# Windowed attention by half-blocks of 64 queries, two heads in one tile, inside a one-core hybrid layer

## The chip, the cores and the metric

The kernel runs on one core of a Trainium2 chip, in one launch. The core has five engines that run at the same time, each through its own instructions in a fixed order: TensorE (PE in the profile; its weight loads are listed apart as PEld), VectorE (DVE), ScalarE (ACT), GpSimd (POOL) and SyncE (SP, which here only issues DMAs). They wait for each other and for DMAs through semaphores. Data lies in SBUF (128 partitions); TensorE writes its results into PSUM. The metric is the time of one execution on the device in microseconds (us). A kernel is timed in several runs and its median is taken; one more execution is profiled, and it has its own time.

## The reference: what is computed

One layer works on 2048 latent tokens and 256 context tokens of width 1024. After a modulated normalisation one projection makes the inputs of two groups of heads: a retention of 4 heads, in chunks of 128 tokens in both directions, and an attention of 8 heads of width 64 over 2 key/value heads. An output projection, a gate, the residual and a last normalisation follow. The change is in the attention:

```python
def windowed_gqa(q, k, v, k_ctx, v_ctx, sink):
    """Latent queries: one softmax over [sink, all context keys, latent keys within +-WINDOW]."""
    G = Hq // Hkv                                   # 4 query heads share a key/value head
    qb = q.reshape(B, Hkv, G, nb, ATT_BLOCK, dh) * (dh ** -0.5)     # ATT_BLOCK = WINDOW = 128, nb = 16
    kb, vb = band_blocks(k), band_blocks(v)         # block before, own block, block after: 384 keys
    valid = (jnp.abs(qpos - kpos) <= WINDOW) & (kpos >= 0) & (kpos < L)
    s_loc = jnp.where(valid, jnp.einsum('bkgnqd,bknjd->bkgnqj', qb, kb), NEG)
    s_ctx = jnp.einsum('bkgnqd,bkcd->bkgnqc', qb, k_ctx)            # 256 context keys
    p = sink_softmax(jnp.concatenate([s_ctx, s_loc], axis=-1), sink)
    out = p[..., :Lc] @ v_ctx + p[..., Lc:] @ vb    # (einsum)
```

A query at place i of its block sees the keys from i to i+256 of the 384. So the first 64 queries of a block together see keys 0 to 319 and the last 64 see keys 64 to 383.

## The kernel before, in words

**Stages.** Up to about 660 us the kernel loads and modulates the inputs and makes the projections, which it writes to DRAM block by block (a block is 128 tokens): `d_k` keys, `d_v` values, `d_aq` queries, `d_qkv` and `d_st` for the retention, `d_g` gates. Then the last projection (`ag1` of the first four blocks) is interleaved with the attention scores of block 0 and the retention of block 0 (`WEAVE`, about 665 to 686 us). From there to 1142 us runs the block loop: 32 half-blocks t, with block b = t // 2 and key/value head kv = t % 2. The last 7 us finish block 15.

**Precision.** A value is kept as a rounded high part and a low part; the matmuls on them run on float32r (written f32 in the profile, like plain float32). Keys: each of two matmuls (`hl`) takes 128 rows of high and low parts. Transposes and the retention's matmuls are plain float32.

**One head of attention** (`att_head`, lines 713 to 749). With the 128 queries of a head as stationary operand (`AQ[b][:, h, :]`) TensorE makes the scores `S` in four matmuls: line 733 over the keys of the window in `kwin` (384 columns, 256 for blocks 0 and 15), line 737 over the 256 context keys `kctx`, each for two parts. `S` is one PSUM tile (`pS`, one buffer): the next head's scores wait until VectorE has read it. VectorE adds the mask and takes the maximum (line 739, 640 columns), ScalarE takes the exponential with its sum (line 746), and `att_norm` multiplies by the reciprocal on GpSimd (line 755) in `pb`, which holds the four heads of one kv.

**From p to the output** (`att_t`, `att_v`, lines 1186 to 1208). For each of five tiles of 128 keys (three of the window, two of the context: X and Y) TensorE transposes the four heads' probabilities (line 1193, four transposes into one PSUM bank `pt`), ScalarE makes the high part (line 1195), VectorE the low part (line 1196), both in the tile `phl` (two buffers), and TensorE multiplies with the values in two matmuls of 512 columns into `o` (line 1206). `att_out` adds the two parts of the values and multiplies by the gate, and `proj` (line 1243, tiles `pz`) is the output projection, from `mr` (retention) and `ma` (attention).

**The order** of the block loop is written out in two strings, `STEPS`, for kv = 0 and 1: a0 to a3 are the heads of the next half-block (t + 1), N their norms, T and V transposes and value matmuls of this one, o pieces of the projection, s/S, R, Y, U, q the retention of block b + 1 and its parts (`Y` writes `yt`, whose product with the gate tile `gr` becomes `mr`). t = 0 has a string of its own, `FIRST`, without heads. A list scheduler then places the instructions of each engine, the DMA issues of SP among them; it follows the strings except where it takes an operand to be late.

**Loads.** `kwin` has three slots, block b in slot b % 3; `load_kv(b + 2)` stands at the start of half-block 2b + 1, and the slot of kv is free when the last head of kv that reads the old block is done. `load_att` loads the queries of a block in four DMAs (128 KB each, runs of 512 bytes) into `aq`, two buffers. `first` holds block 0's retention inputs; `fw` is the last norm's weight.

## Time and profile before

| | |
|---|---|
| runs | 1152.22, 1150.06, 1148.82 us; median 1150.06 |
| the profiled execution | 1151.04 us, its span in the profile 1149.2 us |
| TensorE clock granted | 0.991 of full speed over the span |
| PE busy | 1129.1 us (98%), 6319 matmul records |
| PEld, DVE, ACT, POOL busy | 976.0 (85%), 786.7 (68%), 475.8 (41%), 328.3 us (29%) |
| window scores (line 733) | 224 records of 384 columns, 32 of 256 |
| context scores (line 737) | 256 records of 256 columns |
| transposes of p (line 1193) | 624 records |
| value matmuls (line 1206) | 312 records of 512 columns |

How to read it: PE's matmuls are pipelined, so a record's duration (say 338 ns) is longer than the distance to the next record's start; what a matmul costs is read from the starts of neighbours in a timeline. "Idle before" is the time in which an engine waited, with what ended it. The share of an engine is a mean over stages, so the stage in question has to be read by itself.

### The profile page before, as it was taken

How to read it: one execution, taken by the hardware profiler on the slowest of the kernel's cores; microseconds unless marked ns; L12 is line 12 of the kernel's file. 1: busy time of each engine (PE TensorE's matmuls, PEld its weight loads, DVE VectorE, ACT ScalarE, POOL GpSimd, SP SyncE). 2: the span in 40 equal slices, each digit the busy share in tenths (PEclk: the TensorE clock that was granted, in tenths of full speed). 3: DMA queues.
4: the chain of work that ended last, by engine and by line, in shares of the span. 5: the costliest groups of instructions: out<-in, count | busy, mean ns of one | idle time of the engine just before them, and what ended most of it. 6: DMA issues, size and time to landing. Idle time of an engine off the chain costs nothing.

```text
span 1149.2 us, 18100 instructions
## 1 busy us (share of the span) xinstructions
PE 1129.1 (98%) x6319; PEld 976.0 (85%) x6319; DVE 786.7 (68%) x1907; ACT 475.8 (41%) x1044; POOL 328.3 (29%) x459
## 2 busy tenths in 40 slices
PE   8999999999999999999999999999999999999997
PEld 5887879989978889998888877888888888888885
DVE  6973994665674545656657357777777777777774
ACT  4344522332453002322111156555555555555553
POOL 0000020100011200001104343555555555555553
PEclk8999999999999999999999999999999999999999
DMA  8948893374674532543356276344444444444310
GB/s 319 340 152 263 290 282 132 116 256 126 203 230 137 154 109 83 178 123 113 101 162 210 79 188 223 116 133 134 133 133 134 133 134 133 133 133 134 97 56 37
DMA packets 139537, 182.25 MB, mean 159 GB/s; under 512 B 11315, under 2 KB 103091, under 8 KB 139318
## 3 DMA queue, kind: packets, MB, share of 16 engines
q1 hardware_dynamic: 124372, 173.46, 48.0%
q10 hardware_dynamic: 15074, 7.64, 2.2%
q8 instruction: 50, 0.82, 0.3%
q14 instruction: 41, 0.34, 0.1%
HBM read 130.19 MB, written 50.86 MB: 158 GB/s over the span
## 4 chain that ended last, share of the span: by engine, by line
PE 81%; DVE 7%; issue 5%; DMA 4%; ACT 2%; POOL 1%; SPq 0%; POOLq 0%; DVEq 0%; ACTq 0%
PE pz L1243 14%; PE rv L344 8%; PE rk L331 7%; PE o L1206 6%; PE ag L331 6%; PE pt L1193 5%; PE aq L331 5%; PE rg L331 4%; PE rq L331 4%; PE S L733 3%; PE S L737 2%; PE u L460 2%; PE ak L331 2%; PE av L331 1%; DVE wss L205 1%
## 5 line engine op out<-in xcount | busy, mean ns | idle before, releaser
L746 ACT ACTIVATE p<-p,m 128x641 f32<-128x641 f32 (+1 forms) x128 | 104.6, 817 | 62.1 <-DVE m L743 61.8
L755 POOL TENSOR_SCALAR p<-p,m 128x640 f32<-128x640 f32 (+1 forms) x128 | 101.7, 794 | 87.5 <-DVE m L754 86.2
L1195 ACT ACTIVATE phl<-pt 128x512 fp32r<-128x512 f32 x156 | 92.6, 595 | 78.1 <-PE pt L1193 76.0
L1196 DVE TENSOR_TENSOR phl<-pt,phl 128x512 fp32r<-128x512 f32 x156 | 106.3, 683 | 24.1 <-ACT phl L1195 23.4
L739 DVE CUSTOM_DVE_ANT_0 p<-S,msk 128x640 f32<-128x640 f32 (+1 forms) x128 | 102.5, 801 | 13.4 <-PE S L737 6.6
L1243 PE MATMUL pz<-wg1h,ma 128*128 128x512 f32 x256 | 106.1, 419 | 0.1
L1243 PE MATMUL pz<-wg0h,mr 128*128 128x512 f32 x256 | 103.6, 409 | 0.6 <-DVE mr L113 0.6
L1193 PE MATMUL pt<-ident,p 128*128 128x128 f32 x624 | 93.2, 272 | 0.0
L1193 PEld LDWEIGHTS pt<-ident,p 128*128 128x128 f32 x624 | 75.3, 140 | 8.4
L733 PE MATMUL S<-kwin,aq 128*128 128x384 f32 (+1 forms) x256 | 79.4, 332 | 0.1
L436 ACT ACTIVATE vw<-v,wdec 128x128 fp32r<-128x128 f32 x128 | 43.7, 394 | 84.2 <-DVE v L449 84.2
L737 PE MATMUL S<-kctx,aq 128*128 128x256 f32 x256 | 71.1, 281 | 0.0
L1206 PE MATMUL o<-phl,vwin 128*128 128x512 f32 x184 | 62.2, 416 | 1.3 <-DVE phl L1196 0.8
L1243 PEld LDWEIGHTS pz<-wg0h,mr 128*128 128x128 f32 x256 | 48.1, 188 | 9.2 <-DVE mr L113 0.9
L1243 PEld LDWEIGHTS pz<-wg1h,ma 128*128 128x128 f32 x256 | 48.2, 188 | 7.8 <-POOL ma L1221 0.5
L733 PEld LDWEIGHTS S<-kwin,aq 128*128 128x128 f32 x256 | 48.0, 188 | 6.9 <-DVE m L739 1.6
L737 PEld LDWEIGHTS S<-kctx,aq 128*128 128x128 f32 x256 | 48.2, 188 | 5.2
L1243 PE MATMUL pz<-wg0l,mr 128*128 128x512 f32 x128 | 50.6, 395 | 0.0
L1243 PE MATMUL pz<-wg1l,ma 128*128 128x512 f32 x128 | 50.3, 393 | 0.0
L438 DVE SCALAR_TENSOR_TENSOR vw<-v,wdec,vw 128x128 fp32r<-128x128 f32 x128 | 40.2, 358 | 6.7 <-ACT vw L436 6.7
L1217 DVE TENSOR_TENSOR mf<-o,ob 64x256 f32<-64x256 f32 x64 | 26.7, 417 | 24.4 <-ACT ob L1214 23.8
L1206 PE MATMUL o<-phl,vctx 128*128 128x512 f32 x128 | 41.6, 404 | 0.2 <-DVE phl L1196 0.2
(425 smaller groups left out, 3015.3 us busy)
## 6 DMA issues: line engine op xcount, KB each, us to landing
wss<-in_wss SPq DMA_DIRECT2D x32, 512.0 KB, 6.1
qkv<-d_qkv SPq DMA_DIRECT2D x15, 768.0 KB, 4.8
aq<-d_aq SPq DMA_DIRECT2D x64, 128.0 KB, 3.5
xb<-in_xn SPq DMA_DIRECT2D x16, 512.0 KB, 3.7
out<-xb SPq DMA_DIRECT2D x31, 256.0 KB, 4.9
st<-d_st SPq DMA_DIRECT2D x15, 512.0 KB, 6.8
d_g<-g ACTq DMA_DIRECT2D x28, 256.0 KB, 2.8
x<-in_xt SPq DMA_DIRECT2D x12, 512.0 KB, 5.7
```

The source lines that it names most:

```text
L331: pe.matmul(ps, w[:, a, k, c0 : c0 + P], ht[b][:, k, :], start=(k == 0 and i == 0), stop=(k == NK - 1 and i == 2),)
L344: pe.matmul(ps, ht[a][:, k, t * P : (t + 1) * P], w[:, b, k, :], start=(k == 0 and i == 0), stop=(k == NK - 1 and i == 2),)
L733: i = pe.matmul(psc[:, o:512].rearrange("p (s t) -> p s t", t=P), AQ[b][:, h, :], C2["kwin"][:, kv, hl, ksel], start=(hl == 0), stop=(hl = ...
L737: pe.matmul(psc[:, 512:768], AQ[b][:, h, :], C2["kctx"][:, kv, hl], start=(hl == 0), stop=(hl == 1))
L739: dve.tensor_tensor_reduce(out=pb[:, j, 0:n], in0=psc[:, o : o + n], in1=mk, op0=ALU.add, op1=ALU.max, scale=1.0, scalar=-3e38, accum_out= ...
L746: act.activation(pb[:, j, 0 : n + 1], pb[:, j, 0 : n + 1], AF.Exp, bias=m4[:, 1, j : j + 1], scale=0.125, accum_out=m4[:, 2, j : j + 1],)
L755: PE["norm"] = pool.tensor_scalar(pb[:, j, 0:n], pb[:, j, 0:n], m4[:, 2, j : j + 1], 0.0, op0=ALU.mult, op1=ALU.add)
L1193: pe.transpose(ppt[:, j], pb[:, j, kt * P : (kt + 1) * P], ident)
L1195: PE["phl"] = act.activation(phl[:, 0], ppt, AF.Copy)
L1196: PE["low"] = dve.tensor_tensor(phl[:, 1], ppt, phl[:, 0], op=ALU.subtract)
L1206: pe.matmul(PO[kv], vt, PH[kt][:, hl], start=(kt == 0 and hl == 0), stop=(kt == nkt - 1 and hl == 1))
L1243: pe.matmul(PZ[n2], m[:, a, k % RH, :], WG[k // 4][c][:, k % 4, s], start=(k == 0 and i == 0), stop=(k == NK - 1 and i == 2),)
```

## The change

**What it does.** Attention goes by halves of a block: a unit is 64 queries of two heads (128 rows) where it was 128 queries of one head. Per block and kv there are still four units, j = 0 to 3: `sub` = j // 2 is the half, `pair` = j % 2 the pair of heads. A half has the 320 window keys that its queries can see: the own block C, the full neighbour F (128 keys) and half of the other neighbour H (64 keys). So a unit has 576 columns and not 640 (blocks 0 and 15: 448 or 512 where it was 512).

- `kwin` has five slots instead of three, so that the window of a unit is one run of columns; every third block the two blocks that are still needed are loaded again into slots 0 and 1 (four more DMAs of 128 KB). In `load_kv` the values are now loaded first.
- In `att_t` the tiles are C, F, H, X, Y; the H tile takes four transposes of 64 columns each (before: 128), and its high and low parts go into a tile of its own, `phh`, whose upper 64 rows are zero. Blocks 0 and 15 have five tiles, F and H with two transposes each (before: four tiles of four).
- In `att_v` the tiles F and H use other values for each half, so each of their matmuls of 512 columns becomes two of 256. H of the second half needs the last 64 keys of block b - 1 in partitions 0 to 63: `vs`, loaded once a block (`load_vs`, step "v").
- The queries are loaded half by half: eight DMAs of 64 KB a block, with runs of 256 bytes. The mask is a strip `msk` of 2112 columns, the sinks are set by halves of the partitions, twice a kv.
- To make room, `glast` (the last gate before its activation) takes one of the two `aq` buffers. `aq1` then takes the buffer of `aq0` and can be loaded when block 0's last head is done, `aq2` when the gate of `glast` is stored. `fw` is loaded after the weave and not in the tables' stage.

```diff
-    "a0 o0 O T0 o1 a1 N0 T1 R F0 F1 V0 a2 N1 T2 B V1 o2 a3 N2 T3 o3 V2 o4 T4 r2 N3 o5 V3 o6 V4 o7",
+    "a0 o0 O T0 o1 a1 N0 T1 R F0 F1 V0 a2 N1 T2 B V1 o2 a3 N2 T3 o3 V2 v o4 T4 r2 N3 o5 V3 o6 V4 o7",
 ...
+    def window(b, sub):
+
+        w = [("F", 0, P), ("C", P, P), ("H", 2 * P, 64)] if sub == 0 else [("H", 64, 64), ("C", P, P), ("F", 2 * P, P)]
+        return w[(b == 0) : 3 - (b == NB - 1)]
+
+    def columns(b, sub):
+
+        at, n = {}, 0
+        for name, _, m in window(b, sub):
+            at[name] = (n, m)
+            n += m
+        return {**at, "X": (n, P), "Y": (n + P, P)}, n + CTX
 ...
-    def load_kv(b):
-        if b >= NB:
-            return
+    def load_keys(s, b, n):
         for kv in range(2):
             for dup in range(2):
                 nc.sync.dma_start(
-                    C2["kwin"][64 * dup : 64 * dup + 64, kv, :, b % 3, :].bitcast(F32),
-                    d_k[kv, :, :, b * P : (b + 1) * P].rearrange("s d t -> d s t"),
+                    C2["kwin"][64 * dup : 64 * dup + 64, kv, :, s * P : (s + n) * P].bitcast(F32),
+                    d_k[kv, :, :, b * P : (b + n) * P].rearrange("s d t -> d s t"),
                 )
-        v = C2["pool"].tile([P, 2, P], F32R, tag="v", name=f"vwin{b}", bufs=4)
-        nc.sync.dma_start(v.bitcast(F32), d_v[b])
-        VW[b] = v
+
+    def load_kv(b):
+
+        w = (b - 1) % 3
+        if b < NB:
+            v = C2["pool"].tile([P, 2, P], F32R, tag="v", name=f"vwin{b}", bufs=4)
+            nc.sync.dma_start(v.bitcast(F32), d_v[b])
+            VW[b] = v
+        if w == 0 and b > 1 and b <= NB:
+            load_keys(0, b - 2, 2)
+        if b < NB:
+            load_keys(w + 2 if b else 1, b, 1)
+
+    def load_vs(b):
+
+        if b < NB:
+            nc.sync.dma_start(C2["vs"][0:64].bitcast(F32), d_v[b - 1, 64:P])
 ...
-        AQ[b] = C2["pool"].tile([P, AH, P], F32R, tag="aq", name=f"aq{b}")
-        for i in range(4):
-            nc.sync.dma_start(
-                AQ[b][32 * i : 32 * i + 32].bitcast(F32), d_aq[b, i].rearrange("g (j d) t -> d (g j) t", d=32)
-            )
+
+        AQ[b] = C2["pool"].tile([P, 2, AH, 64], F32R, tag="aq", name=f"aq{b}")
+        for sub in range(2):
+            for i in range(4):
+                nc.sync.dma_start(
+                    AQ[b][32 * i : 32 * i + 32, sub].bitcast(F32),
+                    d_aq[b, i, :, :, 64 * sub : 64 * sub + 64].rearrange("g (j d) t -> d (g j) t", d=32),
+                )
 ...
-        slots = window(b)[0]
-        nl = len(slots) * P
+        sub, pair = j // 2, j % 2
+        win = window(b, sub)
+        nl = sum(m for _, _, m in win)
         n = nl + CTX
         o = 512 - nl
-        h = 4 * kv + j
-        ksel = {0: slice(0, 2), NB - 1: slice(0, 3, 2)}.get(b, slice(0, 3))
-        m0 = mask_at(b)
-        mk = C2["msk"][:, m0 : m0 + n // P].rearrange("p s t -> p (s t)")
+        c0 = b % 3 * P + win[0][1]
 ...
-            pool.tensor_copy(PB[(b, kv)][0][:, :, n], sink8[:, 4 * kv : 4 * kv + 4])
+        if pair == 0:
+            pool.tensor_copy(pb[:, j : j + 2, n], sink8[:, 2 * kv : 2 * kv + 2])
+        h = 2 * kv + pair
+        q = AQ[b][:, sub, 2 * h : 2 * h + 2].rearrange("p h t -> p (h t)")
 ...
         for hl in range(2):
-            i = pe.matmul(
-                psc[:, o:512].rearrange("p (s t) -> p s t", t=P),
-                AQ[b][:, h, :], C2["kwin"][:, kv, hl, ksel], start=(hl == 0), stop=(hl == 1),
-            )
-            pe.matmul(psc[:, 512:768], AQ[b][:, h, :], C2["kctx"][:, kv, hl], start=(hl == 0), stop=(hl == 1))
+            i = pe.matmul(psc[:, o:512], q, C2["kwin"][:, kv, hl, c0 : c0 + nl], start=(hl == 0), stop=(hl == 1))
+            pe.matmul(psc[:, 512:768], q, C2["kctx"][:, kv, hl], start=(hl == 0), stop=(hl == 1))
 ...
-        fw = new("fw", [P, D])
-        nc.sync.dma_start(fw, fnw)
 ...
-        new("glast", [P, 2, GT])
+        C2["glast"] = c2.tile([P, 2, GT], F32, tag="aq", name="glast")
 ...
-    fw, vctx = C2["fw"], C2["vctx"]
+    vctx = C2["vctx"]
+    fw = s2.tile([P, D], F32, name="fw", bufs=1)
+    nc.sync.dma_start(fw, fnw)
+
+
+    for n, shape in (("vs", [P, 2, P]), ("phh", [P, 2, 4, P])):
+        C2[n] = s2.tile(shape, F32R, name=n, bufs=1)
+        pool.memset(C2[n].bitcast(F32), 0.0)
 ...
+    TILES = "CFHXY"
+
+    def halves_of(b, kt):
+
+        return [sub for sub in range(2) if TILES[kt] in columns(b, sub)[0]]
 ...
-        for j in range(4):
-            pe.transpose(ppt[:, j], pb[:, j, kt * P : (kt + 1) * P], ident)
-        phl = s2.tile([P, 2, 4, P], F32R, tag="phl", name=f"phl{b}_{kv}_{kt}", bufs=2)
-        PE["phl"] = act.activation(phl[:, 0], ppt, AF.Copy)
-        PE["low"] = dve.tensor_tensor(phl[:, 1], ppt, phl[:, 0], op=ALU.subtract)
+        subs = halves_of(b, kt)
+        for sub in subs:
+            c, m = columns(b, sub)[0][TILES[kt]]
+            for j in (2 * sub, 2 * sub + 1):
+                pe.transpose(ppt[:m, j], pb[:, j, c : c + m], ident)
+        phl = C2["phh"] if m < P else s2.tile([P, 2, 4, P], F32R, tag="phl", name=f"phl{b}_{kv}_{kt}", bufs=2)
+        js = slice(2 * subs[0], 2 * subs[-1] + 2)
+        PE["phl"] = act.activation(phl[:m, 0, js], ppt[:m, js], AF.Copy)
+        PE["low"] = dve.tensor_tensor(phl[:m, 1, js], ppt[:m, js], phl[:m, 0, js], op=ALU.subtract)
 ...
-        slots = window(b)[0]
-        nkt = len(slots) + 2
         if kt == 0:
             PO[kv] = bank(f"o{b}_{kv}", "o")
-        vt = VW[slots[kt][1]][:, kv, :] if kt < len(slots) else vctx[:, kt - len(slots), kv, :]
-        for hl in range(2):
-            pe.matmul(
-                PO[kv], vt, PH[kt][:, hl], start=(kt == 0 and hl == 0), stop=(kt == nkt - 1 and hl == 1)
-            )
+        t = TILES[kt]
+        if t in "CXY":
+            vt = VW[b][:, kv, :] if t == "C" else vctx[:, "XY".index(t), kv, :]
+            uses = [(vt, slice(0, 4))]
+        else:
+            near = {("F", 0): lambda: VW[b - 1], ("F", 1): lambda: VW[b + 1], ("H", 0): lambda: VW[b + 1],
+                    ("H", 1): lambda: C2["vs"]}
+            uses = [(near[(t, sub)]()[:, kv, :], slice(2 * sub, 2 * sub + 2)) for sub in halves_of(b, kt)]
+        for vt, js in uses:
+            for hl in range(2):
+                pe.matmul(
+                    PO[kv][:, js], vt, PH[kt][:, hl, js], start=(kt == 0 and hl == 0), stop=(kt == 4 and hl == 1)
+                )
```

**How it moves instructions.** In the rows below a name is the tile written, with block and kv or tile number, `<-`, the operands, and partitions x columns; xN are N equal rows in a run.

TensorE in half-block 0, after the transposes of block 0's first kv (`o0_0` their value matmuls, `pz0` the projection from `mr0`, `S1` scores of block 1). Before:

```order
L1206 MATMUL o0_0_6481<-phl0_0_2_6489,vctx_6030 128x512 x2
L1206 MATMUL o0_0_6481<-phl0_0_3_6503,vctx_6030 128x512
L733 MATMUL S1_1_6575<-kwin_6005,aq1_6449 128x384
L737 MATMUL S1_1_6575<-kctx_6017,aq1_6449 128x256
L733 MATMUL S1_1_6575<-kwin_6005,aq1_6449 128x384
L737 MATMUL S1_1_6575<-kctx_6017,aq1_6449 128x256
L1206 MATMUL o0_0_6481<-phl0_0_3_6503,vctx_6030 128x512
L1243 MATMUL pz0_0_6551<-wg0h_5749,mr0_6470 128x512
L1243 MATMUL pz0_0_6551<-wg0l_5750,mr0_6470 128x512
L1243 MATMUL pz0_1_6667<-wg0h_5749,mr0_6470 128x512
L1243 MATMUL pz0_1_6667<-wg0l_5750,mr0_6470 128x512
L733 MATMUL S1_2_6610<-kwin_6005,aq1_6449 128x384
```

And now:

```order
L1263 MATMUL o0_0_6503<-phl0_0_3_6522,vctx_6043 128x512 x2
L1263 MATMUL o0_0_6503<-phl0_0_4_6532,vctx_6043 128x512 x2
L1304 MATMUL pz0_0_6584<-wg0h_5751,mr0_6494 128x512
L1304 MATMUL pz0_0_6584<-wg0l_5752,mr0_6494 128x512
L1304 MATMUL pz0_1_6697<-wg0h_5751,mr0_6494 128x512
L1304 MATMUL pz0_1_6697<-wg0l_5752,mr0_6494 128x512
L1304 MATMUL pz0_0_6584<-wg0h_5751,mr0_6494 128x512 x2
L1304 MATMUL pz0_0_6584<-wg0l_5752,mr0_6494 128x512
L1304 MATMUL pz0_0_6584<-wg0h_5751,mr0_6494 128x512 x2
L1304 MATMUL pz0_0_6584<-wg0l_5752,mr0_6494 128x512
L1304 MATMUL pz0_0_6584<-wg0h_5751,mr0_6494 128x512 x2
L1304 MATMUL pz0_0_6584<-wg0l_5752,mr0_6494 128x512
```

The heads S1_1 and S1_2 (and S1_0, which stood ahead of pt0_0_0) are gone from here. Behind the last row come s1, the transposes of kv 1 and y1; S1_0_0 stands after y1, and S1_0_1 to S1_1_3 follow, the last four with three to six other rows between two of them.

TensorE around the third tile's transposes of a half-block in the middle (block 9, kv 1; now `pt9_1_2` are the H transposes). Before:

```order
L1193 MATMUL pt9_1_2_9697<-ident_66,p9_1_9433 128x128 x4
L1206 MATMUL o9_1_9684<-phl9_1_1_9663,vwin10_9259 128x512 x2
L1243 MATMUL pz9_0_9624<-wg0h_5749,mr9_9529 128x512
L1243 MATMUL pz9_0_9624<-wg0l_5750,mr9_9529 128x512
L1243 MATMUL pz9_0_9624<-wg0h_5749,mr9_9529 128x512
L733 MATMUL S10_3_9721<-kwin_6005,aq10_9261 128x384
```

And now:

```order
L1243 MATMUL pt9_1_2_9862<-ident_66,p9_1_9589 64x128 x4
L1263 MATMUL o9_1_9848<-phl9_1_1_9827,vwin8_8686 128x256 x2
L1263 MATMUL o9_1_9848<-phl9_1_1_9827,vwin10_9398 128x256 x2
L1304 MATMUL pz9_0_9788<-wg0h_5751,mr9_9685 128x512
L1304 MATMUL pz9_0_9788<-wg0l_5752,mr9_9685 128x512
L1304 MATMUL pz9_0_9788<-wg0h_5751,mr9_9685 128x512
L767 MATMUL S10_0_3_9887<-kwin_6007,aq10_9408 128x320
```

The second tile's two value matmuls of 512 columns have become four of 256 at the same place; the next head follows three projection matmuls later, as before, now with 320 columns. Every tile F and H of blocks 1 to 14 goes like this.

SP's queue around the keys of block 6 (`vs` and `kwin` the loads of the change, `gr6` the gate tile that takes the buffer of `gr4`). Before:

```order
L660 DMA kwin_6005<-d_k_62 64x2x128 x2
L665 DMA vwin6_7887<-d_v_63 128x256
L712 DMA xb4_7552<-in_xn 128x1024
L709 DMA ga5_7894<-d_g_64 128x512
L676 DMA st5_7783<-d_st_65 128x1024
L660 DMA kwin_6005<-d_k_62 64x2x128 x2
L696 DMA aq6_7889<-d_aq_61 32x8x128
L682 DMA gr6_7785<-d_g_64 128x512
L696 DMA aq6_7889<-d_aq_61 32x8x128 x3
```

And now:

```order
L701 DMA qkv6_7799<-d_qkv_60 128x1536
L745 DMA xb4_7630<-in_xn 128x1024
L706 DMA st5_7866<-d_st_65 128x1024
L712 DMA gr6_7868<-d_g_64 128x512
L686 DMA vwin6_7970<-d_v_63 128x256
L676 DMA kwin_6007<-d_k_62 64x2x128 x4
L728 DMA aq6_7976<-d_aq_61 32x8x64 x8
```

Before, the four key loads of a block stood in two pairs: kv 0 ahead of `vwin`, kv 1 ahead of `aq` and `gr`. Now the four of block 6 stand together behind `gr6`. So do those of blocks 4 (with the four loads of 128 KB) and 5; from block 8 on they stand ahead of `gr`, and for block 7 `gr7` stands between the two of kv 0.

More of the change, by code (lines that the diff above doesn't have):

```diff
@@ L282, in decays @@
         dve.tensor_tensor(lg, t8, u8, op=ALU.subtract)
-        dve.tensor_scalar(nsink, pr[:, 8:16], -1.0, None, op0=ALU.mult)
-        dve.tensor_scalar(sink8, pr[:, 8:16], 8.0, None, op0=ALU.mult)
+        for i in range(2):
+            rows = slice(64 * i, 64 * i + 64)
+            dve.tensor_scalar(nsink[rows], pr[rows, 8 + i : 16 : 2], -1.0, None, op0=ALU.mult)
+            dve.tensor_scalar(sink8[rows], pr[rows, 8 + i : 16 : 2], 8.0, None, op0=ALU.mult)
         for h in range(RH):
@@ L833, in new @@
             return C2[n]
-        new("kwin", [P, 2, 2, 3, P], F32R)
+        new("kwin", [P, 2, 2, 5 * P], F32R)
         load_kv(0)
@@ L852, in tables @@
             nc.sync.dma_start(vctx[:, t].bitcast(F32), d_v[NB + t])
-        fw = new("fw", [P, D])
-        nc.sync.dma_start(fw, fnw)
-        msk = new("msk", [P, 14, P], BF16)
+        msk = new("msk", [P, MASKL[1] + P + 64 + CTX], BF16)
         pool.memset(msk, 0.0)
-        for i, o in enumerate(MASKS):
-            if o != 1:
-                dve.tensor_copy(msk[:, i], tb[1][:, o // 2])
-        new("glast", [P, 2, GT])
+        for name, sub, _, _, o, n in parts:
+            for b, first_ in ((1, MASK0[sub]), (NB - 1, MASKL[sub])):
+                at = columns(b, sub)[0].get(name)
+                if at:
+                    dve.tensor_copy(msk[:, first_ + at[0] : first_ + at[0] + n], tri[:, o : o + n])
+        C2["glast"] = c2.tile([P, 2, GT], F32, tag="aq", name="glast")
         dmat = new("dmat", [P, RH, P])
```

55 lines of the change are left out of this document (31 added, 24 removed).

## The prediction

> **What bounds the kernel now.** I read the windows by stage first, then the waits, then single rows of the timeline. In the block loop the windows are, in columns: stretch, its length, busy time and count of PE, PEld, DVE, ACT and POOL, the granted clock, DMA share and GB/s.
>
> ```profile
> 700.00:800.00 100.00, 99.13 (x603) 87.70 (x604) 76.71 (x228) 56.55 (x115) 52.70 (x76) 1.00 0.44 135
> 800.00:900.00 100.00, 100.00 (x610) 88.78 (x610) 80.13 (x232) 60.77 (x126) 55.52 (x78) 1.00 0.44 132
> ```
>
> TensorE is busy without a hole, at full clock, and VectorE, the next, is at 80%. So in the loop an instruction of TensorE counts in full, and time saved on another engine counts for nothing while TensorE does not wait for it. Where it does wait is the way into the loop (the waits of PE from 660 to 712 us: total, times, longest):
>
> ```profile
> PE s L780 <- DMA first<-d_qkv: 1.3, 1, 1.3
> PE y L788 <- DVE m L754: 1.0, 1, 1.0
> PE pz L1243 <- DVE mr L113: 0.6, 1, 0.6
> PE o L1206 <- DVE phl L1196: 0.5, 2, 0.2
> PE o L1206 <- ACT phl L1195: 0.4, 1, 0.4
> ```
>
> These 3.8 us are all there is to win or lose by order. A matmul's price is the distance between starts, here one head, four transposes and three projection matmuls:
>
> ```profile
> 747.49 0.34 PE L733 MATMUL S<-kwin,aq 128*128 128x384 f32 x1
> 747.67 0.28 PE L737 MATMUL S<-kctx,aq 128*128 128x256 f32 x1
> 747.79 0.34 PE L733 MATMUL S<-kwin,aq 128*128 128x384 f32 x1
> 747.96 0.28 PE L737 MATMUL S<-kctx,aq 128*128 128x256 f32 x1
> 748.08 0.60 PE L1193 MATMUL pt<-ident,p 128*128 128x128 f32 x4
> 748.43 0.48 PE L1243 MATMUL pz<-wg1h,ma 128*128 128x512 f32 x1
> 748.75 0.39 PE L1243 MATMUL pz<-wg1l,ma 128*128 128x512 f32 x1
> 748.98 0.40 PE L1243 MATMUL pz<-wg1h,ma 128*128 128x512 f32 x1
> ```
>
> 384 columns cost 0.175 us (mean of 0.18 and 0.17), 256 cost 0.12 (over many such pairs 0.117), 512 cost 0.23. From the first transpose to the second 512 are 0.67 us: 0.231 for the first 512 leaves 0.109 for a transpose. A head costs 0.59 us.
>
> **The change part by part.**
>
> *Scores.* The two groups that set the counts here and for the transposes:
>
> ```profile
> L733 PE MATMUL S<-kwin,aq 128*128 128x384 f32 x224 | 70.8, 338 | 0.0
> L1193 PE MATMUL pt<-ident,p 128*128 128x128 f32 x624 | 93.2, 272 | 0.0
> ```
>
> 224 matmuls go from 384 to 320 columns, half way between 0.117 and 0.175, so 0.146: 224 x 0.029 = **-6.5 us**. In blocks 0 and 15 sixteen matmuls go from 256 to 192 columns. No row shows this type under 256 columns. By the line 192 would cost 0.09, which saves 0.4; at the other bound the matmul runs like the plain f32 passes of the retention, which go twice over their operands at 0.11 us for 128 columns each (rows below), so 192 cost 0.33: +3.4 us. The nearest row is the 256-column one, so I stay near the lower end and take **+0.5**.
>
> *Values.* In 28 half-blocks the tiles F and H have eight matmuls of 256 for four of 512: 8 x 0.117 against 4 x 0.231 is 0.012 us, hence +0.3; with a spread of 0.12 for a 256, at most +1.0. I take **+0.4**. Blocks 0 and 15 do in five tiles what they did in four, with as many columns.
>
> *Transposes.* There are as many as before, but 120 of them (4 in each of 28 half-blocks, 2 in four) have 64 stationary columns, with the same 128 moving ones (`ident`). Nothing in the trace has 64. What holds a transpose at 0.109 us?
>
> ```profile
> 843.27 0.39 PE L788 MATMUL y<-st,qd 128*128 128x128 f32 x2
> 843.49 0.39 PE L789 MATMUL y<-st,qd 128*128 128x128 f32 x2
> 100.35 0.47 PE L168 MATMUL ss_xc<-ones,sqc 128*128 128x1 f32 x3
> 100.68 0.47 PE L331 MATMUL rg<-h2h,wrg 128*128 128x512 f32 x1
> L1193 PEld LDWEIGHTS pt<-ident,p 128*128 128x128 f32 x624 | 75.3, 140 | 8.4
> L1243 PEld LDWEIGHTS pz<-wg0h,mr 128*128 128x128 f32 x256 | 48.1, 188 | 9.2 <-DVE mr L113 0.9
> ```
>
> Plain f32 passes of 128 moving columns are 0.11 apart (two in 0.22), and so are three passes of one single moving column (0.33): for those the load of the 128 stationary columns alone takes 0.11. But the load of a transpose is another one: its record is 140 ns where others have 188, so it is some 50 ns shorter, and if it takes 0.06 it cannot hold the transpose at 0.109. Then the moving columns do, and these stay 128: **0**. If the load holds it after all, half the columns save up to 0.053 each: 120 x 0.053 = -6.4 us. This is a rival below.
>
> The Trainium skill, page "TensorE: Matmul & The Clock Gate", section "LDWEIGHTS (loading the stationary operand)", lets the load take the stationary columns divided by 1.2 GHz, an estimate of 107 ns for 128 and 53 for 64. The one-column passes agree with it (0.11), the shorter record of the transposes speaks against it there. By that rule the sum below would be 6.4 us lower.
>
> *Other engines.*
>
> ```profile
> L739 DVE CUSTOM_DVE_ANT_0 p<-S,msk 128x640 f32<-128x640 f32 (+1 forms) x128 | 102.5, 801 | 13.4 <-PE S L737 6.6
> L746 ACT ACTIVATE p<-p,m 128x641 f32<-128x641 f32 (+1 forms) x128 | 104.6, 817 | 62.1 <-DVE m L743 61.8
> L1196 DVE TENSOR_TENSOR phl<-pt,phl 128x512 fp32r<-128x512 f32 x156 | 106.3, 683 | 24.1 <-ACT phl L1195 23.4
> ```
>
> The mask, the exponential and the norm on GpSimd shrink by a tenth, 128 times each: some 10 us on each of three engines, all under TensorE's 100%, so 0; they only make later waits less likely. The extra sinks and the two memsets stand on GpSimd at 55%: 0.
>
> *Loads in the loop.* Per block four more query DMAs, one `vs`, and every third block four of 128 KB for the keys. The queue's rows around the end of an even half-block:
>
> ```profile
> 747.38 0.69 DVE L1229 TENSOR_TENSOR gr<-yt,gr 128x512 f32<-128x512 f32 x1
> 748.86 1.30 POOL L1232 TENSOR_TENSOR mr<-gr,mr 128x512 fp32r<-128x512 f32 x1
> 748.15 1.23 SPq L660 DMA_DIRECT2D kwin<-d_k  x2
> 750.19 0.33 SPq L682 DMA_DIRECT2D gr<-d_g  x1
> 750.57 1.41 SPq L696 DMA_DIRECT2D aq<-d_aq  x3
> 753.32 0.34 PE L733 MATMUL S<-kwin,aq 128*128 128x384 f32 x1
> kwin<-d_k SPq DMA_DIRECT2D x52, 64.0 KB, 2.3
> aq<-d_aq SPq DMA_DIRECT2D x52, 128.0 KB, 3.5
> ```
>
> `gr` waits for GpSimd's `mr` (750.16) and now the keys of blocks 4, 5 and 6 stand behind it. After `gr` come `vwin` (0.33, some 0.1 to the next) and two key DMAs of 0.62: the second is issued at 751.3 and lands 2.3 later, at 753.6, while the next half-block's first scores stand at 753.32. For blocks 4 and 5 TensorE's order has put these scores much later (S3_0_0 and S4_0_0 stand behind y3 and most of y4, 2.7 us and more), for block 7 one pair is ahead; so only S5_0_0 meets it: **+0.4**, no gain possible; with the whole DMA late, 2. Queries are loaded a block ahead of use and eight issues of 0.47 with 3.5 to landing end long before: 0, and without that cover each late microsecond would stand on TensorE 14 times. `vs` waits for the H matmuls of the odd half and is wanted half a half-block later, about 10 us against 2.4: 0.
>
> *The way into the loop.* S0_0_0 waits for the first loads; four more query DMAs (0.47 each) ahead of them make it later by 1 to 2 us, which the 1.3 us wait for `first` absorbs, since `fw` (512 KB) is no longer ahead of `first`: 0, between -1.3 and +1.
>
> Then come the heads of block 1:
>
> ```profile
> 686.05 0.33 PE L733 MATMUL S<-kwin,aq 128*128 128x384 f32 x1
> 686.61 1.65 ACT L814 ACTIVATE first<-first,ra 128x128 f32<-128x128 f32 x4 [3.01 <-DVE ra L807]
> 689.55 0.43 SPq L682 DMA_DIRECT2D gr<-d_g  x1
> 696.01 0.33 PE L733 MATMUL S<-kwin,aq 128*128 128x384 f32 x1
> 696.79 0.83 DVE L739 CUSTOM_DVE_ANT_0 p<-S,msk 128x640 f32<-128x640 f32 x1 [0.40 <-PE S L737]
> 700.87 0.46 PE L788 MATMUL y<-sfw,qd 128*128 128x128 f32 x2 [0.96 <-DVE m L754]
> ```
>
> Before, three heads stood ahead of y1 (from 686.05). Now none does. The time to y1 hardly shortens by their 1.8 us where the wait is for ACT's line 814 (until 688.26), but the two masks no longer stand ahead of `mr` and of the low parts on DVE, nor the norms ahead of y1's `qd` on GpSimd. I put y1 1.6 us earlier than 700.87, with 1.1 us less of TensorE's rows done by then (the three heads gone, more projection done): **-0.5**. The queries of block 1 are issued behind `gr1` (690.0), six of 0.47, so by 692.8, and land 3.5 us later; S1_0_0 stands some 3 us behind y1, at 702: no wait.
>
> The heads then follow each other closely. A head's turn, from its first score to the end of its mask, took 1.61 us (696.01 to 697.62); with 64 columns less 1.47. From S1_1_0 to S1_1_1 there are 1.09 us of TensorE's rows, to S1_1_2 0.86: 0.4 and 0.6 are missing. S3_0_0 to S3_1_0 and S4_0_0 to S4_0_3 stand 1.55 to 1.7 apart, enough for the mask but not always for a low part (683 ns) as well: 0.8 more. Together **+1.8**. After S5 the spacing is that of before.
>
> *Sum:* -6.5 + 0.5 + 0.4 + 0 + 0.4 - 0.5 + 1.8 = -3.9. From the profiled execution's 1151.0 that gives 1147.1; the median of the runs lies 1.0 lower than that execution, so 1146.1 in the same terms. I say **1146.5**.
>
> **The rivals.**
>
> *Half transposes cost half.* For it: an f32 load of 128 columns is seen to hold 0.11 us, and the transposes stand at 0.109. Against it: their load record is shorter. It adds -6.4 (-4.8 if the last of each four is still held by the next matmul's load): 1140.
>
> *The backlog costs more (the slower side).* The heads of blocks 1, 3 and 4 are held by VectorE's whole turn, mask, two small instructions and a low part (about 0.75 + 0.3 + 0.68) behind the scores, 2.2 us instead of 1.47. Fourteen gaps from S1_0_0 to S4_0_3 are shorter than that, by 8.3 us together. For it: VectorE at 80% has no room to do twice its heads. Against it: the low parts can go first or wait in their two buffers. Price 8.3 for 1.8: +2.6, so 1152.7 by the median; it decides once more than 5.7 of the 8.3 are paid, and with 192 columns at the upper bound as well it is 1155.6.
>
> *The gain is given back without loss:* 192 columns at the upper bound (+2.9 over my value) or keys late in several blocks, 3 us: about 1149.5.
>
> **How the numbers follow.** Forecast 0.47, half transposes 0.28, given back 0.13, backlog 0.12. The range for 8 in 10 goes from the rival below, 1139.5, to the backlog, 1153; the forecast's own is 1144 to 1149. A difference of 0.3%, 3.4 us, is what this measurement can tell from none. Faster by more: the half transposes and somewhat over half of the forecast, 0.53. Within: the rest of the forecast, the gain given back and half of the backlog, 0.35. Slower: 0.12.
>
> **What would show it.** Scores of 320 columns 0.146 apart, and 192 not far above 0.1. H transposes spaced 0.109: right; 0.06: the rival. PE's waits from 660 to 720 us in sum 4 to 7 us, the new ones at lines 767 and 768 from DVE; a wait of S5_0_0 for `kwin` of about half a microsecond, and none for `aq` or `vs`. From 820 us on PE at 100% as before. The prediction is wrong where PE waits for keys in every block, or where VectorE's share in the loop does not fall below 80%.

## The result, and the profile after

The changed kernel takes **1157.9 us** (median of four runs, 1157.36 to 1158.69), the kernel before 1150.2 us beside it. The ratio is **1.0071**, interval 1.0058 to 1.0083: slower by 0.7%. The prediction was 1146.5, range 1139.5 to 1153. It was wrong, and on the wrong side.

The loss has one place. Below is the table by stage of the changed kernel, with the columns of the prediction's first view (stretch, its length, busy time and count of PE, PEld, DVE, ACT, POOL, then clock, DMA share, GB/s):

```profile
690.00:720.00 30.00, 27.69 (x158) 21.57 (x158) 18.55 (x53) 16.05 (x31) 10.26 (x16) 1.00 0.74 230
720.00:780.00 60.00, 56.56 (x351) 48.23 (x352) 44.04 (x130) 32.23 (x67) 31.17 (x48) 1.00 0.40 124
780.00:840.00 60.00, 58.59 (x371) 50.96 (x371) 46.45 (x138) 33.99 (x72) 30.99 (x48) 1.00 0.45 139
840.00:900.00 60.00, 60.00 (x388) 53.60 (x387) 47.32 (x144) 36.04 (x77) 31.16 (x49) 1.00 0.47 146
```

In the kernel before the two middle stretches were:

```profile
720.00:780.00 60.00, 60.00 (x366) 53.22 (x365) 47.70 (x141) 35.93 (x74) 33.12 (x47) 1.00 0.44 132
780.00:840.00 60.00, 60.00 (x369) 53.35 (x368) 47.55 (x137) 35.35 (x72) 33.17 (x47) 1.00 0.47 138
```

So PE was full from 720 us on, and now it is full only from 840 us on. (Its count of matmuls is higher there, 388 in 60 us for 367 before, mainly because eight value matmuls of 256 columns stand where four of 512 stood.) To put the loss into blocks I use the first transpose `yt` of each block, which stands at the same place of the program in all kernels, and the time from one to the next, each from the one profiled execution:

| us | `yt` 0 at | 0 to 1 | 1 to 2 | 2 to 3 | 3 to 5 | 5 to 15 | 15 to end | span |
|---|---|---|---|---|---|---|---|---|
| before | 687.2 | 29.9 | 28.8 | 28.8 | 57.7 | 287.8 | 29.0 | 1149.2 |
| after | 686.8 | 32.7 | 31.9 | 31.4 | 59.6 | 284.8 | 29.8 | 1156.9 |

Up to block 0 nothing is lost (-0.3). From block 0 to block 5 it is +10.2, from block 5 to block 15 -3.0 (a block of the loop is 28.46 where it was 28.83), and behind the last `yt` +0.8: together the 7.7 of the spans. So the static gain is there, block by block, and the first five blocks eat it up three times over.

What PE waited for from 665 to 845 us (total, times, longest):

```profile
PE pt L1243 <- POOL p L786: 1.8, 3, 1.1
PE S L767 <- DVE m L770: 1.6, 4, 0.6
PE S L767 <- DMA kwin<-d_k: 1.4, 2, 0.8
PE o L1263 <- DVE mf L1275: 0.9, 1, 0.9
PE o L1263 <- DVE phl L1247: 0.7, 3, 0.2
PE o L1263 <- ACT phl L1246: 0.6, 1, 0.6
PE pz L1304 <- DVE mr L114: 0.6, 1, 0.6
PE pz L1304 <- DVE mr L1293: 0.5, 1, 0.5
PE yt L1288 <- ACT first L845: 0.5, 1, 0.5
```

These rows are 8.6 us; before, all waits of that stretch were 3.8. The new ones are TensorE waiting for the heads' own chain: the mask's maximum (VectorE), the norm (GpSimd), the sum of the parts (VectorE). A wait also costs more than its length. The longest one, with the three transposes ahead of it:

```profile
727.70 0.49 PE L1243 MATMUL pt<-ident,p 128*128 128x128 f32 x3
729.33 0.33 PE L1243 MATMUL pt<-ident,p 128*128 128x128 f32 x1 [1.14 <-POOL p L786]
```

From the first of the three to the fourth it is 1.63 us, where transposes 0.11 apart take 0.33: 1.30 lost for a wait of 1.14.

The first head of block 1 stood at 686.05 before. Now (its row, and the view of the tile `aq` from 684 to 696 us, which holds only the eight loads of `aq1`):

```profile
704.27 0.31 PE L767 MATMUL S<-kwin,aq 128*128 128x320 f32 x1
...
L728 SPq DMA_DIRECT2D aq<-d_aq x8: 303/507/957, 684.6 to 694.6; - x8
...
DMA to landing us min/median/max: 1.9/5.6/7.7
```

The queries were issued from 684.6 to 694.6, and the last landing on record is at 699.3 (two of the eight have none on record). The head does not wait for them: it stands at 704.27 because in PE's order it stands behind y1, the retention of block 1. Two different things are thus late: the queries, and the order.

### The profile page after: what moved, and what is told of

It reads as the page before. It is cut to its first block, busy times and chain, and to the rows that moved or that the text cites. A ratio compares the mean times of both kernels' runs of the same rounds, so it can differ in the third digit from the quotient of the medians.

```text
span 1156.9 us, 18517 instructions
## 1 busy us (share of the span) xinstructions
PE 1130.2 (98%) x6438; PEld 974.5 (84%) x6439; DVE 782.7 (68%) x1914; ACT 469.5 (41%) x1048; POOL 328.7 (28%) x493
## 4 chain that ended last, share of the span: by engine, by line
PE 73%; DVE 10%; issue 6%; POOL 4%; DMA 3%; ACT 3%; SPq 1%; POOLq 0%; ACTq 0%; DVEq 0%
PE pz L1304 12%; PE rv L347 8%; PE rk L334 7%; PE ag L334 5%; PE o L1263 5%; PE aq L334 5%; PE pt L1243 4%; PE rg L334 4%; PE rq L334 4%; PE S L767 3%; PE S L768 2%; PE u L463 2%; PE ak L334 2%; PE av L334 1%; DVE wss L206 1%
## 5 line engine op out<-in xcount | busy, mean ns | idle before, releaser
L777 ACT ACTIVATE p<-p,m 128x577 f32<-128x577 f32 (+2 forms) x128 | 98.1, 766 | 72.0 <-DVE m L774 71.0
L786 POOL TENSOR_SCALAR p<-p,m 128x576 f32<-128x576 f32 (+2 forms) x128 | 95.8, 749 | 91.6 <-DVE m L785 84.2
L770 DVE CUSTOM_DVE_ANT_0 p<-S,msk 128x576 f32<-128x576 f32 (+2 forms) x128 | 94.3, 737 | 18.3 <-PE S L768 13.4
L1247 DVE TENSOR_TENSOR phl<-pt,phl 128x512 fp32r<-128x512 f32 x128 | 86.7, 680 | 27.6 <-ACT phl L1246 25.4
L1246 ACT ACTIVATE phl<-pt 128x512 fp32r<-128x512 f32 x128 | 75.1, 589 | 72.0 <-PE pt L1243 70.2
L1243 PE MATMUL pt<-ident,p 128*128 128x128 f32 (+1 forms) x624 | 95.4, 273 | 2.0 <-POOL p L786 1.8
L1243 PEld LDWEIGHTS pt<-ident,p 128*128 128x128 f32 (+1 forms) x624 | 74.4, 134 | 13.1 <-POOL p L786 3.4
L767 PE MATMUL S<-kwin,aq 128*128 128x320 f32 (+2 forms) x256 | 73.9, 310 | 3.6 <-DVE m L770 2.1
L767 PEld LDWEIGHTS S<-kwin,aq 128*128 128x128 f32 x256 | 48.1, 188 | 12.4 <-DVE m L770 4.5
L1263 PE MATMUL o<-phl,vwin 128*128 128x512 f32 (+1 forms) x184 | 45.2, 345 | 2.6 <-DVE phl L1247 1.0
```

Of the source, the lines that this page charges most:

```text
L767: i = pe.matmul(psc[:, o:512], q, C2["kwin"][:, kv, hl, c0 : c0 + nl], start=(hl == 0), stop=(hl == 1))
L770: dve.tensor_tensor_reduce(out=pb[:, j, 0:n], in0=psc[:, o : o + n], in1=mask(b, sub), op0=ALU.add, op1=ALU.max, scale=1.0, scalar=-3e38, ...
L777: act.activation(pb[:, j, 0 : n + 1], pb[:, j, 0 : n + 1], AF.Exp, bias=m4[:, 1, j : j + 1], scale=0.125, accum_out=m4[:, 2, j : j + 1],)
L786: PE["norm"] = pool.tensor_scalar(pb[:, j, 0:n], pb[:, j, 0:n], m4[:, 2, j : j + 1], 0.0, op0=ALU.mult, op1=ALU.add)
L1243: pe.transpose(ppt[:m, j], pb[:, j, c : c + m], ident)
L1246: PE["phl"] = act.activation(phl[:m, 0, js], ppt[:m, js], AF.Copy)
```

## The experiments

The ratio of each run is to the kernel before, timed on the same chip; the rounds ran on different chips, so between rounds the ratios are to be compared, not the times. "By the table" means the columns `0 to 1`, `1 to 2`, `2 to 3` and `3 to 5` above, in this order (six numbers: `5 to 15` and `15 to end` as well). S1_0_0 is the first unit of the scores of block 1, key/value head 0.

### First round: the shared buffer, or the key loads?

The two candidates were the buffer that `glast` takes from the queries, and the eight key loads of every third block. Run 1 gives `glast` its own tile; for its 4 KB the padded tile `phh` had to go, so run 2 has that second edit alone.

```diff
-        C2["glast"] = c2.tile([P, 2, GT], F32, tag="aq", name="glast")
+        new("glast", [P, 2, GT])
 # runs 1 and 2: no phh, and vs on 64 rows
-        phl = C2["phh"] if m < P else s2.tile([P, 2, 4, P], F32R, tag="phl", ...)
+        phl = s2.tile([P, 2, 4, P], F32R, tag="phl", ...)
-                    PO[kv][:, js], vt, PH[kt][:, hl, js],
+                    PO[kv][:, js], vt[:m], PH[kt][:m, hl, js],     # m = 64 for H
```

> The changed kernel with two edits: `glast` has a tile of its own again, so `aq1` need not wait for block 0's heads nor `aq2` for the store of the gate; and, to find its 4 KB, the H tile uses the common `phl` and its value matmuls take 64 rows, so that the padded tile `phh` is gone. Theory A (the shared buffer): all that is lost between the first `yt` of block 0 (686.8, 0.3 us ahead of the kernel before) and that of block 5 (842.3, 9.9 us behind), with the gain of five blocks some 12 us, comes from the queries of block 1 being late and VectorE's and GpSimd's work with them, the later order of blocks 2 to 5 included. Then S1_0_0 stands at about 687 (704.3 now), `yt` of block 5 at 831 to 833, and the time is 1145 to 1147. Theory B (the key loads: eight at once in every third block, behind `gr`): only the loss up to block 1, some 3 us, comes back: 1154 to 1156, with the waits of S3, S4 and S5 as they are.

Measured: 1159.8 us, ratio 1.0087 (1.0073 to 1.0101).

> The second edit of that kernel alone: H's value matmuls on 64 rows, no `phh`, `glast` still in a buffer of the queries. Both theories: no change against the changed kernel, 1156.5 to 1159. If 64 rows are cheaper or dearer than 128 padded ones for TensorE (8 matmuls of 256 columns in a half-block's F and H, 4 of them H, at 0.117 us), it shows as a spacing other than 0.117 and as up to 120 x 0.06 = 7 us.

Measured: 1168.8 us, ratio 1.0173 (1.0154 to 1.0192). Both times fell outside what either theory gave, since the edit meant as a filler costs some 11 us by itself (below, run 8). Taken against each other, the own tile is worth 9.0 us, and by the table the first head of block 1 is back at 686.0 and the blocks take 29.6, 30.3, 30.0, 58.5 in place of 32.9, 31.9, 32.7, 60.5.

Runs 3 and 4 put one part each into the kernel before: the shared buffer, and the loads (five slots, the change's `load_keys` and `load_kv`, `fw` later).

```diff
 # run 3
-        new("glast", [P, 2, GT])
+        C2["glast"] = c2.tile([P, 2, GT], F32, tag="aq", name="glast")
 # run 4, beside load_keys and load_kv
-        new("kwin", [P, 2, 2, 3, P], F32R)
+        new("kwin", [P, 2, 2, 5 * P], F32R)
-                AQ[b][:, h, :], C2["kwin"][:, kv, hl, ksel], ...
+                AQ[b][:, h, :], C2["kwin"][:, kv, hl, c0 : c0 + nl], ...     # c0 = (b % 3 + (b == 0)) * P
```

> The kernel before with one line of the change: `glast` takes one of the two `aq` buffers. Keys, heads and values are those of before. Theory A: block 1's heads stand behind y1 as in the changed kernel (S1_0 from 686.1 to about 703), VectorE is in arrears, and the kernel is slower by 3 to 7 us: 1153 to 1157. Theory B: the lateness is taken up by VectorE's reserve of 20%, at most +2: 1150 to 1152.

Measured: 1150.3 us, ratio 1.0007 (0.9997 to 1.0017).

> The kernel before with the loads of the change alone: five slots of keys, two blocks of keys loaded again in every third block (four DMAs of 128 KB), values ahead of the keys, `fw` loaded after the weave; the order on TensorE stays that of before. (The mask has 9 tiles in place of 14, since the window's blocks now stand in order.) Theory A: 1149 to 1151, with at most 0.5 us of waits for `kwin`. Theory B: waits for `kwin` or `aq` in blocks 3 to 5 and behind, slower by 4 us or more: 1154 and up.

Measured: 1149.3 us, ratio 0.9997 (0.9987 to 1.0008). The key loads cost nothing: by the table 29.9, 28.8, 28.8, 57.7, as before. But neither does the shared buffer in the kernel before (30.4, 28.8, 28.8, 57.7): there the first head of block 1 also comes late, at 698.6, near the end of y1, and 0.5 us is lost in that block and nothing behind it. So theory A did not hold as I had put it. Something else has to come with the sharing.

### Second round: the sharing with the eight query loads

Run 5 leaves the changed kernel as it is, but finds 4 KB for `glast` elsewhere: `junk` is a throw-away of the last norm that nobody needs before block 1.

```diff
-        C2["glast"] = c2.tile([P, 2, GT], F32, tag="aq", name="glast")
+        C2["glast"] = c2.tile([P, 2, GT], F32, tag="junk", name="glast", bufs=1)
-        junk = s1.tile([P, D], F32, tag="junk", name=f"junk{b}", bufs=1)
+        junk = C2["pool"].tile([P, D], F32, tag="junk", name=f"junk{b}", bufs=1)
```

> The changed kernel with one edit: `glast` takes the buffer of `junk` (a throw-away of the last norm, 4 KB, first used in block 1), which moves from the pool `s1` into the tables' pool; the query loads get both `aq` buffers as before the change, and `phh` stays with its 128 rows. Theory A (the shared buffer makes the loss): S1_0_0 at about 686, `yt` of block 5 at 831 to 833, a block of 28.46 us in the loop, and 1143 to 1147. Theory B (the loss lies in the half-block units themselves or their key loads): 1152 or more.

Measured: 1147.95 us, ratio 0.9992 (0.9982 to 1.0003). By the table 29.6, 29.7, 29.4, 56.9: 9.9 of the lost us are back, the loop block is 28.46, but the time is 1 us above the forecast; 2 us are still lost in blocks 1 to 3.

Runs 6 and 7 take the queries in halves of 64 (eight DMAs, runs of 256 bytes) into the kernel before, with and without the shared buffer.

```diff
-        for i in range(4):
-            nc.sync.dma_start(AQ[b][32 * i : 32 * i + 32].bitcast(F32), d_aq[b, i].rearrange(...))
+        for sub in range(2):
+            ts = slice(64 * sub, 64 * sub + 64)
+            for i in range(4):
+                nc.sync.dma_start(AQ[b][32 * i : 32 * i + 32, :, ts].bitcast(F32), d_aq[b, i, :, :, ts].rearrange(...))
```

> The kernel before with two lines of the change: `glast` in one of the `aq` buffers, and the queries of a block in eight DMAs of half a block (runs of 256 bytes). Heads, keys and values are those of before. Theory A1 (the shared buffer alone was 1.4 us; with eight loads, most of them queued behind others, the heads of blocks 1 to 3 come so late and close together that TensorE waits for VectorE and GpSimd): slower by 5 to 9 us, 1154 to 1158. Theory A2 (the shared buffer is dear only with the work of the half-block units): 1149 to 1152.

Measured: 1159.2 us, ratio **1.0089** (1.0071 to 1.0108).

> The kernel before with the queries in eight DMAs of half a block, nothing else. Theory A1: the loads are early enough by themselves, 1148 to 1151. If the eight loads alone are the cause, it stands where the run with both lines stands, 1154 to 1158.

Measured: 1150.3 us, ratio 1.0006 (0.9997 to 1.0014). So each of the two lines costs about 1 us by itself (0.07% and 0.06%), which this measurement does not tell from nothing, and both together cost 10, with full heads of 128 queries and 384 keys. That is a loss of the size of the changed kernel's, made without its attention. The stage table of run 6 and its new waits:

```profile
720.00:780.00 60.00, 55.92 (x329) 47.00 (x329) 45.16 (x132) 33.21 (x69) 30.30 (x43) 1.00 0.38 117
780.00:840.00 60.00, 60.00 (x368) 53.38 (x367) 47.74 (x140) 36.70 (x77) 32.37 (x47) 1.00 0.45 137
```

```profile
PE pt L1196 <- POOL p L758: 3.0, 4, 1.6
PE S L736 <- DVE m L742: 2.0, 4, 1.3
```

The same two waits as after the change, GpSimd's norm and VectorE's maximum; by the table 34.0, 31.5, 31.4, 57.7. The first head of block 1 stands at 708.4, in run 3 (shared, four loads) at 698.6.

Run 8 is run 5 with the H tile's value matmuls on 64 rows, to see what the filler had cost.

```diff
-                    PO[kv][:, js], vt, PH[kt][:, hl, js],
+                    PO[kv][:, js], vt[:m], PH[kt][:m, hl, js],     # m = 64 for H, else 128
```

> The kernel of the first of these runs, with the H tile's value matmuls on 64 rows in place of 128 padded ones; `phh` stays a tile of its own. If the matmuls of 64 rows are what cost (a switch from 128 rows to 64 and back held TensorE by 0.10, 0.11 and 0.08 us in the second run's trace), it is slower than that kernel by 9 to 12 us. If the cost was the shared `phl`, it is within 1.5 us of it.

Measured: 1158.9 us, ratio 1.0087 (1.0074 to 1.0099), 10.9 us above run 5. The 64 rows cost it, not the buffer. TensorE around H's matmuls in run 5, and then in run 8:

```profile
905.62 0.39 PE L1304 MATMUL pz<-wg0h,mr 128*128 128x512 f32 x1
905.85 0.40 PE L1263 MATMUL o<-phh,vwin 128*128 128x256 f32 x2
906.08 0.40 PE L1263 MATMUL o<-phh,vs 128*128 128x256 f32 x2
906.32 0.40 PE L1304 MATMUL pz<-wg0h,mr 128*128 128x512 f32 x1
906.55 0.40 PE L1304 MATMUL pz<-wg0l,mr 128*128 128x512 f32 x1
```

```profile
912.04 0.40 PE L1306 MATMUL pz<-wg0h,mr 128*128 128x512 f32 x1
912.37 0.50 PE L1265 MATMUL o<-phh,vwin 64*128 64x256 f32 x2
912.71 0.40 PE L1265 MATMUL o<-phh,vs 64*128 64x256 f32 x2
913.04 0.50 PE L1306 MATMUL pz<-wg0h,mr 128*128 128x512 f32 x1
913.37 0.40 PE L1306 MATMUL pz<-wg0l,mr 128*128 128x512 f32 x1
```

From the first row to the last it is 0.93 with 128 padded rows and 1.33 with 64: four steps of 0.1 around the change of rows and back. 28 half-blocks times 0.40 are 11.2 us, close to the measured 10.9.

### Third round: the order or the lateness?

Late queries can cost in two ways: the heads wait for them, or the scheduler, which takes them to be late, writes the heads far behind and close together. Run 10 keeps the shared buffer, and with it the late queries, but holds TensorE's instructions of half-blocks 1 to 5 in the order of the strings (the scheduler then places the other queues around that). Run 9 does it for half-blocks 2 to 5 on top of run 5, for its last 2 us. Every matmul and transpose goes through `pin`:

```diff
+        def pin(self, i):
+            return tc.keep_in_program_order(i) if self.on else i
 ...
+        pe.on = 1 <= t <= 5            # run 10; run 9: 2 <= t <= 5
```

Run 10:

> The changed kernel, `glast` still in a buffer of the queries and the queries still late, with TensorE's instructions of half-blocks 1 to 5 held in the order of `STEPS`. Theory P (the order written for late queries costs more than the lateness): the first head of block 1 waits for `aq1` until about 699, 3 to 5 us in one wait, and the rest follows as in the kernel before: 1149 to 1153. Theory L (the lateness itself costs it, by VectorE's and GpSimd's arrears, in any order): 1156 to 1160.

Measured: **1148.5 us**, ratio 0.9992 (0.9982 to 1.0002): 0.8%, some 9 us, below the changed kernel, from holding the order, with queries as late as they were (the last landing on record stands 12.9 us behind the first `yt`, 12.4 in the changed kernel). SP issues the same loads in the same sequence in both kernels up to about 740 us, so up to there only the order on the engines differs: TensorE's is held, and those of the others are placed around it. What PE waits for at the entry, and the matmuls behind it:

```profile
693.17 2.05 PE L1189 MATMUL s<-qkv 128*128 128x128 f32 x8 [1.43 <-DMA qkv<-d_qkv]
696.40 0.61 PE L1189 MATMUL S<-kwin,aq 128*128 128x320 f32 x1 [1.18 <-DMA aq<-d_aq]
...
697.50 0.63 PE L1189 MATMUL pz<-wg0h,mr 128*128 128x512 f32 x1
697.92 0.63 PE L1189 MATMUL pz<-wg0l,mr 128*128 128x512 f32 x1
698.35 0.63 PE L1189 MATMUL pz<-wg0h,mr 128*128 128x512 f32 x1
```

By the table 33.9, 28.5, 28.7, 56.9. So with the order held the lateness costs some 4 us (33.9 for 29.9 before; part of it is the lower clock of the last section), all in block 0 to 1, and from 700 to 845 us the trace shows no wait of TensorE. What the changed kernel lost from block 1 to 5 (122.8 for 114.1 here) was the order; 1.2 us of that it had saved in block 0 to 1 (32.7 for 33.9). Theory L (no order helps) fell. Theory P had the cause, but not the form: in place of one wait of 3 to 5 us there are two shorter ones, one of them for the retention's inputs (`qkv`).

Run 9:

> The kernel with `glast` in the buffer of `junk`, and TensorE's instructions of half-blocks 2 to 5 held in the order of the strings `STEPS`, so that the heads of blocks 2 and 3 stand where they stood in the kernel before (there the scheduler had put S2_0_0 and S2_0_1 side by side in front of y2, and S3_0_1 inside y3). Theory P (the 2 us that are still lost between block 1 and block 3 come from the order alone; the queries of block 2 had landed at 705 us and were used at 725): TensorE waits for nothing between 705 and 1090 us, `yt` of block 5 comes 145.3 to 145.8 us behind that of block 1's half (block 0's `yt` to block 5's 143.4 to 144 in place of 145.7), and 1145 to 1146.5. Theory Q (VectorE cannot follow there in any order): 1147.5 to 1149, with waits for `m` or `phl` at other places.

Measured: 1148.6 us, ratio 0.9995 (0.9985 to 1.0004): no gain over run 5, a miss for theory P. The loss moved, and the trace names it:

```profile
723.18 0.39 PE L1189 MATMUL S<-kwin,aq 128*128 128x320 f32 x1 [0.83 <-DMA kwin<-d_k]
727.26 0.41 PE L1189 MATMUL S<-kwin,aq 128*128 128x320 f32 x1 [1.48 <-DVE m L770]
```

Block 1 to 2 now takes 31.8. The heads of block 2 wait for keys of block 3, which SP issues at 720, behind `gr2`. (In run 10 and in the changed kernel these keys had gone out at the entry, while the queries were held up.)

Run 11 is run 9 with block 15 in four tiles again:

> The first of these kernels, with block 15 back to four tiles: its second half takes the whole neighbour block 14 (64 masked keys more, 256 columns in place of 192 in eight matmuls, +0.24 us), so that F has four transposes and the H tile is gone. The time from the last `yt` to the end was 29.0 us in the kernel before and 29.8 in the changed one and in that with `glast` in `junk`. If the fifth tile makes that, this kernel ends 0.6 to 1.2 us before the first; if not, 0 to 0.3 behind it.

Beside the window below, the second half of block 15 gets a mask strip of 512 columns, and its F takes the values of block 14.

```diff
-        return w[(b == 0) : 3 - (b == NB - 1)]
+        if b == NB - 1:
+            return [("F", 0, P), ("C", P, P)]
+        return w[(b == 0) :]
```

Measured: 1148.7 us, ratio 0.9995 (0.9985 to 1.0004), the same as run 9. From block 5 to the last `yt` it takes 283.9 us in place of 284.6, and behind it 30.0 in place of 29.8. The fifth tile is not what makes the end 0.8 us longer; what does, stays open.

### Last run: all of it together

Run 12 is run 9 with the loads of the keys and values of blocks 2 and 3 ahead of the block loop; the five slots have room for them.

```diff
     load_att(1)
+    load_kv(2)
+    load_kv(3)
     for t in range(2 * NB):
 ...
-            load_kv(b + 2)
+            if b > 1:
+                load_kv(b + 2)
```

> `glast` in the buffer of `junk`, TensorE's half-blocks 2 to 5 held in the order of `STEPS`, and the keys and values of blocks 2 and 3 loaded before the block loop (five slots have room for them). In the run without this last edit the first heads of block 2 waited 0.8 us for keys that SP issued at 720, behind `gr2`, and the next head 1.5 us for VectorE: 3.0 us lost from `yt` of block 1 to that of block 2. Theory P (that loss is the keys' place in the queue): both waits are gone, block 2 takes 28.5 us in place of 31.8, and the time is 1145 to 1146.5, faster than both kernels. Theory Q (VectorE's arrears): the wait only moves, 1148 to 1149.

Measured: **1144.3 us**, ratio **0.9960** (0.9946 to 0.9975), faster than both kernels, and 0.7 us under theory P's range. Its stage table:

```profile
690.00:720.00 30.00, 29.03 (x179) 24.60 (x178) 23.60 (x69) 19.21 (x38) 15.33 (x22) 1.00 0.58 202
720.00:780.00 60.00, 60.00 (x391) 53.81 (x390) 47.43 (x140) 35.01 (x73) 33.44 (x55) 1.00 0.50 155
```

By the table 29.2, 28.5, 28.5, 56.9, 284.6, 29.8: PE is full from 720 us on, as in the kernel before (from 700 to 845 us no wait of TensorE is on record), and from the first `yt` to the last the loop is 5.4 us shorter (427.6 for 433.0). Run 9's time had been what theory Q gave, but its reason, VectorE's arrears, fell here: with the keys there in time VectorE follows. Whether the order still has to be held once the keys are early, no run shows, since run 5 with the early keys alone is not among them.

## Why the prediction was wrong, step by step

**Scores: right.** In the changed kernel's loop, and in block 0 for 192 columns:

```profile
906.87 0.30 PE L767 MATMUL S<-kwin,aq 128*128 128x320 f32 x1
907.01 0.28 PE L768 MATMUL S<-kctx,aq 128*128 128x256 f32 x1
907.12 0.31 PE L767 MATMUL S<-kwin,aq 128*128 128x320 f32 x1
907.27 0.28 PE L768 MATMUL S<-kctx,aq 128*128 128x256 f32 x1
...
669.43 0.25 PE L767 MATMUL S<-kwin,aq 128*128 128x192 f32 x1
669.51 0.30 PE L768 MATMUL S<-kctx,aq 128*128 128x256 f32 x1
```

0.14 and 0.15 for 320 columns (0.146 forecast), 0.08 to 0.09 for 192. The sixteen of 192 columns therefore saved 0.4 to 0.5 where I had put +0.5: the line through the other sizes held, and the caution towards the plain f32 passes was not needed.

**Values: right.** Four matmuls of 256 columns take 0.47 (905.85 to 906.32 above), two of 512 0.46.

**Transposes: right, the first rival wrong.** Four of 64 stationary columns and, as before, four of 128:

```profile
926.81 0.60 PE L1243 MATMUL pt<-ident,p 128*64 128x128 f32 x4
927.16 0.48 PE L1304 MATMUL pz<-wg1h,ma 128*128 128x512 f32 x1
...
908.09 0.60 PE L1243 MATMUL pt<-ident,p 128*128 128x128 f32 x4
908.45 0.48 PE L1304 MATMUL pz<-wg0h,mr 128*128 128x512 f32 x1
```

0.35 and 0.36 to the next matmul, in both cases 0.109 from one transpose to the next. The load itself got shorter (111 ns in its record, 140 for 128 columns), and the pace did not change:

```profile
L1243 PEld LDWEIGHTS pt<-ident,p 128*64 128x64 f32 x120 | 13.1, 111 | 0.8 <-DVE phl L1247 0.2
```

So the load of the stationary columns does not hold the transposes; the moving columns, 128 in both, are what the prediction named in its place. The rule of the Trainium skill that the prediction weighed (page "TensorE: Matmul & The Clock Gate", section "LDWEIGHTS (loading the stationary operand)") would have taken 6.4 us off; the measurement decides against using it for these transposes.

So the static sum was about right: a block gained 0.37 where 0.44 was forecast, and run 12 has 5.4 us in the loop.

**Loads in the loop: right in size.** S5_0_0 waits 0.64 us for keys (0.4 taken; the prediction's own rows, laid end to end, put the second key load at 751.6 and its landing at 753.9, 0.6 us late, not 753.6), no head waits for `aq`, none for `vs`. Run 4 shows that the five slots cost nothing.

**The way into the loop, and here mainly the backlog: the step that failed.** The prediction saw in the order that the heads of blocks 1, 3 and 4 had been pushed back and close together, and put +1.8 on it. Against run 12, where no head waits behind 700 us, the changed kernel loses 12.4 us from the first `yt` to that of block 5 (155.5 for 143.1; 0.8 of it is the wait of S5_0_0 for keys). Four errors are in this term:

- "These 3.8 us are all there is to win or lose by order" holds for winning only. The waits that an order leaves bound what a better order can win, not what a worse one can lose.
- I priced a head's turn by VectorE's mask alone. GpSimd stood at 0 in "other engines, under TensorE's 100%", yet the waits for its norm are the largest sum among the waits shown above (1.8 us). In two of the three the norm starts when its reciprocal is there, so that mask, exponential and norm stand on the path one after the other. In the longest one the reciprocal was there at 726.6, but GpSimd had the retention's `qd` in front from 725.8 to 728.3, and the norm ran from 728.5 to 729.3: there it was GpSimd's own arrears.
- Each wait was taken at its length; by the distance of starts it cost some 0.2 us more (1.30 for 1.14 above).
- I had y1 1.6 us earlier (-0.5 in the sum), since no mask stood ahead of `mr`. It came at 700.7, where it was before (700.87): PE still waited for `mr` (0.6 and 0.5 us in the waits above).

The slower rival named this mechanism, a place for it and a price of 8.3 at chance 0.12. The mechanism was right, the place too; the price was low by a third, and it named VectorE alone. It should have had most of the chance, since the order was on the table: the one question was whether heads can follow at 1.5 to 1.7 us, and the row of the kernel before said 1.61 for the mask alone. (The chances also don't add up as told: with half of the backlog "within" it is 0.41, and "slower" 0.06, in place of 0.35 and 0.12.)

The sign that was to be watched did not show the loss: TensorE's waits from 660 to 720 us are 4.1 us in sum, within the 4 to 7 forecast, and the other waits lie behind 720 us.

**PE full from 820 us on:** from 840. **The end:** blocks 0 and 15 were put at no loss; behind the last `yt` it is +0.8.
